# Row variance on one core: whole rows per engine and deferred aggregation instead of split rows and a combine chain

## The chip, the core and the metric

The kernel runs on one NeuronCore of a Trainium2 chip. Times are device microseconds of that core, from the start of the program to its end. A profiled execution mostly shows a span 1.7 to 1.9 us shorter than that time. The engines that matter are DVE (VectorE), ACT (ScalarE), POOL (GpSimd), the queue of SP (SyncE), which issues the loads, and the 16 DMA engines that carry them.

## The reference

```python
# x: (32, 512, 1024) float32
mean_sq = np.mean(x**2, axis=-1)
sq_mean = np.mean(x, axis=-1)**2
return (mean_sq - sq_mean).astype(np.float32)
```

This is the variance of each of 16384 rows of 1024 numbers. The input is 67.1 MB and the output 64 KB.

## The kernel before

The rows are spread over 128 partitions, so each partition has 128 rows ("row t" below means 128 rows at once, 512 KB). Row groups arrive in tiles of 1 to 8 rows through five buffers. The groups are small at both ends of the run.

```python
segs = [1, 1, 2, 4] + [8] * 11 + [4] * 5 + [2] * 4 + [1] * 4
xin = ctx.enter_context(tc.tile_pool(name="xin", bufs=5))
...
for si, js in enumerate(segs):
    x_tile = xin.tile([P, JMAX, D], fp32)
    nc.sync.dma_start(out=x_tile[:, 0:js, :], in_=...)
    for j in range(js):
        t = t0 + j
        row = x_tile[:, j, :]
        if t % 2 == 0:      # split row: ACT 656 columns, DVE 368
            nc.scalar.activation(... row[:, 0:GA], func=Square, accum_out=ssqA_buf[:, t:t+1])
            nc.scalar.activation(... row[:, 0:GA], func=Copy,   accum_out=sumA_buf[:, t:t+1])
            nc.vector.bn_stats(out=stats[:, 0, :], in_=row[:, GA:D])
            nc.vector.bn_aggr(out=mv_buf[:, t, :], in_=stats[:, 0:1, :])
        else:               # whole row on DVE
            nc.vector.bn_stats(out=stats[:, 0, :], in_=row[:, 0:HO])
            nc.vector.bn_stats(out=stats[:, 1, :], in_=row[:, HO:D])
            nc.vector.bn_aggr(out=mv_buf[:, t, :], in_=stats)
    # after rows 64 and 112: combine(prev_cp, cp)
nc.sync.dma_start(out=out_v[:, 0:prev_cp], in_=var_buf[:, 0:prev_cp])
combine(prev_cp, T)         # 6 DVE and 2 ACT operations in a chain
nc.sync.dma_start(out=out_v[:, prev_cp:T], in_=var_buf[:, prev_cp:T])
```

`combine` turns DVE's mean and variance of its part, and ACT's sums of the other part, into the variance of the row.

Of the kernel before, what the change touches and what calls it, by code (L numbers as in the profile page):

```python
# [1 line left out]

# [4 lines left out]


@with_exitstack  # L10
def kernel(
    ctx: ExitStack,
    tc: tile.TileContext,
    x: bass.AP,
    out: bass.AP,
):
    nc = tc.nc
    fp32 = mybir.dt.float32
    P = nc.NUM_PARTITIONS

    x_flat = x.flatten_outer_dims()
    N, D = x_flat.shape
    assert N % P == 0
    T = N // P

    xv = x_flat.rearrange("(p t) d -> t p d", t=T)
    out_v = out.rearrange("a b -> (a b)").rearrange("(p t) -> p t", t=T)

    JMAX = 8
    segs = [1, 1, 2, 4] + [8] * 11 + [4] * 5 + [2] * 4 + [1] * 4  # L30
    assert sum(segs) == T

    GA = 656
    NBE = D - GA
    assert NBE <= 512 and NBE % 2 == 0
    HO = D // 2
    assert HO <= 512

    xin = ctx.enter_context(tc.tile_pool(name="xin", bufs=5))
    sq = ctx.enter_context(tc.tile_pool(name="sq", bufs=2))  # L40
    stats_pool = ctx.enter_context(tc.tile_pool(name="stats_pool", bufs=4))
    accs = ctx.enter_context(tc.tile_pool(name="accs", bufs=1))

    sumA_buf = accs.tile([P, T], fp32)
    ssqA_buf = accs.tile([P, T], fp32)
    nbw_buf = accs.tile([P, T], fp32)
    mv_buf = accs.tile([P, T, 2], fp32)
    eb_buf = accs.tile([P, T], fp32)
    ebw_buf = accs.tile([P, T], fp32)
    msqB_buf = accs.tile([P, T], fp32)  # L50
    mw_buf = accs.tile([P, T], fp32)
    ssq_tot = accs.tile([P, T], fp32)
    sum_tot = accs.tile([P, T], fp32)
    sq_mean = accs.tile([P, T], fp32)
    var_buf = accs.tile([P, T], fp32)

    nc.gpsimd.memset(sumA_buf, 0.0)  # L57
    nc.gpsimd.memset(ssqA_buf, 0.0)  # L58
    nbw_v = nbw_buf.rearrange("p (a b) -> p a b", b=2)
    nc.gpsimd.memset(nbw_v[:, :, 0], float(NBE))  # L60
    nc.gpsimd.memset(nbw_v[:, :, 1], float(D))  # L61

    inv_d = 1.0 / D

    def combine(c0, c1):
        sl = slice(c0, c1)
        meanB = mv_buf[:, sl, 0]
        varB = mv_buf[:, sl, 1]
        nc.scalar.activation(  # L69
            out=msqB_buf[:, sl],  # L70
            in_=meanB,
            func=mybir.ActivationFunctionType.Square,
        )
        nc.vector.tensor_add(out=eb_buf[:, sl], in0=varB, in1=msqB_buf[:, sl])  # L74
        nc.vector.tensor_mul(out=ebw_buf[:, sl], in0=eb_buf[:, sl], in1=nbw_buf[:, sl])  # L75
        nc.vector.tensor_add(  # L76
            out=ssq_tot[:, sl], in0=ebw_buf[:, sl], in1=ssqA_buf[:, sl]
        )
        nc.vector.tensor_mul(out=mw_buf[:, sl], in0=meanB, in1=nbw_buf[:, sl])  # L79
        nc.vector.tensor_add(out=sum_tot[:, sl], in0=mw_buf[:, sl], in1=sumA_buf[:, sl])  # L80
        nc.scalar.activation(  # L81
            out=sq_mean[:, sl],
            in_=sum_tot[:, sl],
            func=mybir.ActivationFunctionType.Square,
            scale=inv_d,
        )
        nc.vector.scalar_tensor_tensor(  # L87
            out=var_buf[:, sl],
            in0=ssq_tot[:, sl],
            scalar=inv_d,  # L90
            in1=sq_mean[:, sl],
            op0=mybir.AluOpType.mult,
            op1=mybir.AluOpType.subtract,
        )

    CHECKPOINTS = [64, 112]

    t0 = 0
    prev_cp = 0
    for si, js in enumerate(segs):  # L100
        x_tile = xin.tile([P, JMAX, D], fp32)
        nc.sync.dma_start(  # L102
            out=x_tile[:, 0:js, :], in_=xv[t0 : t0 + js].transpose([1, 0, 2])
        )

        for j in range(js):
            t = t0 + j
            row = x_tile[:, j, :]

            if t % 2 == 0:  # L110
                sq_scr = sq.tile([P, GA], fp32)
                nc.scalar.activation(  # L112
                    out=sq_scr,
                    in_=row[:, 0:GA],
                    func=mybir.ActivationFunctionType.Square,
                    accum_out=ssqA_buf[:, t : t + 1],
                )
                cp_scr = sq.tile([P, GA], fp32)
                nc.scalar.activation(  # L119
                    out=cp_scr,  # L120
                    in_=row[:, 0:GA],
                    func=mybir.ActivationFunctionType.Copy,
                    accum_out=sumA_buf[:, t : t + 1],
                )

                stats = stats_pool.tile([P, 2, nc.vector.BN_STATS_DIM], fp32)
                nc.vector.bn_stats(out=stats[:, 0, :], in_=row[:, GA:D])  # L127
                nc.vector.bn_aggr(out=mv_buf[:, t, :], in_=stats[:, 0:1, :])  # L128
            else:
                stats = stats_pool.tile([P, 2, nc.vector.BN_STATS_DIM], fp32)  # L130
                nc.vector.bn_stats(out=stats[:, 0, :], in_=row[:, 0:HO])  # L131
                nc.vector.bn_stats(out=stats[:, 1, :], in_=row[:, HO:D])  # L132
                nc.vector.bn_aggr(out=mv_buf[:, t, :], in_=stats)  # L133
        t0 += js

        while CHECKPOINTS and t0 >= CHECKPOINTS[0]:
            cp = CHECKPOINTS.pop(0)
            combine(prev_cp, cp)
            prev_cp = cp

    nc.sync.dma_start(out=out_v[:, 0:prev_cp], in_=var_buf[:, 0:prev_cp])

    combine(prev_cp, T)
    nc.sync.dma_start(out=out_v[:, prev_cp:T], in_=var_buf[:, prev_cp:T])


# [1 line left out]
_INS = ['x']  # L148
_OUTS = [((32, 512), 'float32')]


# [23 lines left out]
```

## Time and profile before

| | before |
|---|---|
| time, median of the 5 first runs | 169.03 us (168.85 to 169.26) |
| span of the profiled execution | 167.3 us |
| DVE busy, ACT busy | 73%, 59% |
| last input load landed | 162.07 us |
| last output issued | 164.93 us |

The next lines are from the profile page of the kernel before: busy time of each engine with its share of the span and its instruction count, then the DMA queues (packets, MB, share of 16 engines' span), then the shares of the chain that ended last.

```profile
DVE 121.9 (73%) x338; ACT 98.9 (59%) x263; POOL 0.7 (0%) x8
...
q1 hardware_dynamic: 4320, 67.18, 94.7%
q14 instruction: 5, 0.04, 0.1%
...
DMA 83%; DVE 14%; SPq 1%; issue 0%; DVEq 0%
```

None of the computing engines is full, and the chain is DMA for 83% of its length. The second queue, "q14 instruction", is easy to overlook: five packets of 8192 bytes each, with which engines fetch their next instructions while they run. The trace dates them at 38.0, 47.6, 95.9, 116.3 and 150.6 us.

The next view is the table by stretches of the kernel before. Its columns are the stretch, its length, busy us (and instructions) of DVE, ACT and POOL, the TensorE clock, the mean busy share of the 16 DMA engines, and GB/s.

```profile
20.00:155.00 135.00, 105.34 (x293) 85.16 (x229) 0.00 (x0) 1.00 1.00 429
155.00:157.00 2.00, 1.58 (x5) 1.21 (x4) 0.00 (x0) 1.00 1.02 406
157.00:158.00 1.00, 0.93 (x2) 0.87 (x3) 0.00 (x0) 1.00 0.87 324
158.00:159.00 1.00, 1.00 (x4) 1.00 (x3) 0.00 (x0) 1.00 0.84 332
159.00:160.00 1.00, 0.93 (x4) 1.00 (x4) 0.00 (x0) 1.00 0.66 243
160.00:161.00 1.00, 0.96 (x3) 0.27 (x3) 0.00 (x0) 1.00 0.08 32
161.00:162.00 1.00, 0.72 (x3) 1.00 (x3) 0.00 (x0) 1.00 0.04 16
```

Up to 155 us all 16 DMA engines are busy at 429 GB/s. After 160 us a share of 0.04 to 0.08 remains, which is about one engine of sixteen (1/16 = 0.06). A single engine is still carrying its part of the last rows while 15 have finished.

The end of the timeline of the kernel before follows (start us, duration us, engine, line, operation, output and input). L131 to L133 are the statistics of the last row; L69 to L87 are `combine`; L144 is the output.

```profile
162.09 0.69 DVE L131 BATCH_NORM_STATS2 stats<-x_tile 128x6 f32<-128x512 f32 x1 [0.34 <-DMA x_tile<-in_x_dram]
...
163.42 0.21 DVE L133 BATCH_NORM_AGGREGATE mv_buf<-stats 128x2 f32<-128x12 f32 x1
...
163.66 0.18 DVE L79 TENSOR_TENSOR mw_buf<-mv_buf,nbw_buf 128x16 f32<-128x16 f32 x1
...
164.24 0.18 DVE L75 TENSOR_TENSOR ebw_buf<-eb_buf,nbw_buf 128x16 f32<-128x16 f32 x1
...
164.73 0.17 DVE L87 SCALAR_TENSOR_TENSOR var_buf<-ssq_tot,sq_mean 128x16 f32<-128x16 f32 x1
164.93 0.34 SPq L144 DMA_DIRECT2D out_dram<-var_buf  x1
```

DVE is waiting for the last row (the bracket says so). From there to the output's issue it takes 2.84 us, a chain of DVE operations with two short ACT operations of `combine` in it.

The trace also records when each DMA engine's share of a load landed. The following extract is worked out from those records. It shows four loads of the kernel before: the middle of the 16 engines, the third from last, the second from last, and the last.

```
time order     median   third-last  second-last   last    last minus third-last
one at 62 us    61.71      61.99        62.08     62.41   0.42
one at 102 us  100.57     100.84       100.95    102.23   1.39
rows 120, 121  151.93     152.20       153.01    154.55   2.35
row 127        159.78     160.14       160.54    162.07   1.93
```

One engine falls further and further behind. A tile is usable only when its last engine has landed, so that engine sets the end of the input.

### The profile page before, as it was taken

To read this page: it belongs to the slowest core of one execution; us is meant where nothing else is said; L and a number is where in the kernel's file an instruction comes from. 1 tells how busy PE (TensorE), PEld (TensorE's weight loads), DVE (VectorE), ACT (ScalarE), POOL (GpSimd) and SP (SyncE) were. 2 spreads that over 40 slices of the span, in tenths; PEclk is the share of its full clock that TensorE was granted. 3 is DMA by queue.
4 is the path that set the end of the run, shared out by engine and by line. 5 is a ranking of instruction groups with operands and counts; after the bars stand their busy time and mean duration, and the time that the engine had idled before them with its cause. 6 is when DMAs were issued, how large, how long until landed. Compare 5 with 4: busy or idle time off the path is not lost.

```text
span 167.3 us, 735 instructions
## 1 busy us (share of the span) xinstructions
DVE 121.9 (73%) x338; ACT 98.9 (59%) x263; POOL 0.7 (0%) x8
## 2 busy tenths in 40 slices
DVE  0547149496794949679497965949599997998883
ACT  0637049193773919376492935829289755694761
POOL 1000000000000000000000000000000000000000
DMA  5999898999999999999999999999999999999910
GB/s 183 404 439 478 384 486 384 478 400 433 439 417 462 400 470 392 470 400 454 423 415 462 394 470 392 478 400 449 388 427 427 435 431 427 405 421 410 370 73 2
DMA packets 4325, 67.22 MB, mean 402 GB/s; under 512 B 736, under 2 KB 736, under 8 KB 1504
## 3 DMA queue, kind: packets, MB, share of 16 engines
q1 hardware_dynamic: 4320, 67.18, 94.7%
q14 instruction: 5, 0.04, 0.1%
HBM read 67.11 MB, written 0.07 MB: 402 GB/s over the span
## 4 chain that ended last, share of the span: by engine, by line
DMA 83%; DVE 14%; SPq 1%; issue 0%; DVEq 0%
DMA x_tile<-in_x_dram 83%; DVE stats L132 5%; DVE stats L131 5%; DVE stats L127 3%; DVE mv_buf L133 1%; DVE mv_buf L128 1%; SPq L102 1%; DVE ssq_tot L76 0%; DVE ebw_buf L75 0%; DVE mw_buf L79 0%; DVE var_buf L87 0%; DVE sum_tot L80 0%; DVE eb_buf L74 0%; DVEq L87 0%; DVEq L80 0%
## 5 line engine op out<-in xcount | busy, mean ns | idle before, releaser
L112 ACT ACTIVATE sq_scr<-x_tile 128x656 f32<-128x656 f32 x64 | 47.3, 739 | 56.8 <-DMA x_tile<-in_x_dram 56.7
L127 DVE BATCH_NORM_STATS2 stats<-x_tile 128x6 f32<-128x368 f32 x64 | 34.0, 531 | 40.3 <-DMA x_tile<-in_x_dram 40.2
L119 ACT ACTIVATE cp_scr<-x_tile 128x656 f32<-128x656 f32 x64 | 46.9, 733 | 0.0
L131 DVE BATCH_NORM_STATS2 stats<-x_tile 128x6 f32<-128x512 f32 x64 | 41.9, 654 | 0.9 <-DMA x_tile<-in_x_dram 0.8
L132 DVE BATCH_NORM_STATS2 stats<-x_tile 128x6 f32<-128x512 f32 x64 | 42.3, 661 | 0.0
L133 DVE BATCH_NORM_AGGREGATE mv_buf<-stats 128x2 f32<-128x12 f32 x64 | 12.7, 198 | 0.8
L119 ACT ACTIVATION_READ_ACCUMULATOR cp_scr<-x_tile 128x1 f32 x64 | 11.9, 187 | 0.0
L112 ACT ACTIVATION_READ_ACCUMULATOR sq_scr<-x_tile 128x1 f32 x64 | 11.9, 186 | 0.0
L128 DVE BATCH_NORM_AGGREGATE mv_buf<-stats 128x2 f32<-128x6 f32 x64 | 10.6, 166 | 0.1
L112 ACT ACT_TABLE_LOAD x1 | 1.3, 1283 | 4.5 <-DMA x_tile<-in_x_dram 4.5
L69 ACT ACTIVATE msqB_buf<-mv_buf 128x64 f32<-128x64 f32 (+2 forms) x3 | 0.7, 240 | 3.3 <-DVE mv_buf L133 3.3
L81 ACT ACTIVATE sq_mean<-sum_tot 128x64 f32<-128x64 f32 (+2 forms) x3 | 0.7, 238 | 1.0 <-DVE sum_tot L80 1.0
L87 DVE SCALAR_TENSOR_TENSOR var_buf<-ssq_tot,sq_mean 128x64 f32<-128x64 f32 (+2 forms) x3 | 0.6, 204 | 0.3
L80 DVE TENSOR_TENSOR sum_tot<-mw_buf,sumA_buf 128x64 f32<-128x64 f32 (+2 forms) x3 | 0.6, 203 | 0.3
L79 DVE TENSOR_TENSOR mw_buf<-mv_buf,nbw_buf 128x64 f32<-128x64 f32 (+2 forms) x3 | 0.6, 203 | 0.2
L75 DVE TENSOR_TENSOR ebw_buf<-eb_buf,nbw_buf 128x64 f32<-128x64 f32 (+2 forms) x3 | 0.6, 203 | 0.1
L76 DVE TENSOR_TENSOR ssq_tot<-ebw_buf,ssqA_buf 128x64 f32<-128x64 f32 (+2 forms) x3 | 0.6, 203 | 0.1
L74 DVE TENSOR_TENSOR eb_buf<-mv_buf,msqB_buf 128x64 f32<-128x64 f32 (+2 forms) x3 | 0.6, 197 | 0.0
L57 POOL MEMSET sumA_buf<- 128x128 f32 x1 | 0.2, 205 | 0.3 <-POOLq L159 0.3
L58 POOL MEMSET ssqA_buf<- 128x128 f32 x1 | 0.2, 205 | 0.0
L60 POOL MEMSET nbw_buf<- 128x64 f32 x1 | 0.2, 155 | 0.0
L61 POOL MEMSET nbw_buf<- 128x64 f32 x1 | 0.2, 155 | 0.0
(4 smaller groups left out, 0.4 us busy)
## 6 DMA issues: line engine op xcount, KB each, us to landing
x_tile<-in_x_dram SPq DMA_DIRECT2D x11, 4096.0 KB, 41.8
x_tile<-in_x_dram SPq DMA_DIRECT2D x6, 2048.0 KB, 24.5
x_tile<-in_x_dram SPq DMA_DIRECT2D x5, 1024.0 KB, 14.6
x_tile<-in_x_dram SPq DMA_DIRECT2D x6, 512.0 KB, 6.2
out_dram<-var_buf SPq DMA_DIRECT2D x1, 56.0 KB, 5.4
out_dram<-var_buf SPq DMA_DIRECT2D x1, 8.0 KB, 1.4
```

The lines of the kernel that those rows point to most:

```text
L69: nc.scalar.activation(out=msqB_buf[:, sl], in_=meanB, func=mybir.ActivationFunctionType.Square,)
L74: nc.vector.tensor_add(out=eb_buf[:, sl], in0=varB, in1=msqB_buf[:, sl])
L75: nc.vector.tensor_mul(out=ebw_buf[:, sl], in0=eb_buf[:, sl], in1=nbw_buf[:, sl])
L81: nc.scalar.activation(out=sq_mean[:, sl], in_=sum_tot[:, sl], func=mybir.ActivationFunctionType.Square, scale=inv_d,)
L102: nc.sync.dma_start(out=x_tile[:, 0:js, :], in_=xv[t0 : t0 + js].transpose([1, 0, 2]))
L112: nc.scalar.activation(out=sq_scr, in_=row[:, 0:GA], func=mybir.ActivationFunctionType.Square, accum_out=ssqA_buf[:, t : t + 1],)
L119: nc.scalar.activation(out=cp_scr, in_=row[:, 0:GA], func=mybir.ActivationFunctionType.Copy, accum_out=sumA_buf[:, t : t + 1],)
L127: nc.vector.bn_stats(out=stats[:, 0, :], in_=row[:, GA:D])
L128: nc.vector.bn_aggr(out=mv_buf[:, t, :], in_=stats[:, 0:1, :])
L131: nc.vector.bn_stats(out=stats[:, 0, :], in_=row[:, 0:HO])
L132: nc.vector.bn_stats(out=stats[:, 1, :], in_=row[:, HO:D])
L133: nc.vector.bn_aggr(out=mv_buf[:, t, :], in_=stats)
```

## The change

The change has several parts. Every row now belongs to one engine: ACT has rows 0 to 8 and every third row, DVE has the rest. DVE keeps only raw bn_stats results for most rows, and POOL aggregates them later. For rows from 120 on DVE aggregates straight into the output buffer, so that no combine chain remains behind the last row. Rows 126 and 127 are loaded in halves. The intent is less work on DVE and a shorter end. The diff is cut to its core:

```diff
+    def is_scalar_row(t):
+        return t < 9 or (t % 3 == 2)
...
-    nc.gpsimd.memset(sumA_buf, 0.0)          # and the other buffers of combine
...
+    W = accs.tile([P, 2, T], fp32)           # [:, 0] mean, [:, 1] variance
...
     def combine(c0, c1):                     # now for the ACT rows alone
-        (two ACT and six DVE operations on all rows)
...
+            nc.scalar.activation(out=m2_buf[:, sl], in_=W[:, 0, sl], func=Square)
+            eng = nc.vector if c1 == T else nc.gpsimd
+            eng.tensor_sub(out=var_v[:, sl], in0=msq_buf[:, sl], in1=m2_buf[:, sl])
+    AGG = 120
+    def aggregate(c0, c1):                   # DVE rows, on POOL
+        for r in (0, 1):
+            (13 POOL operations on rows r, r+3, ...)
...
-    CHECKPOINTS = [64, 112]
+    CHECKPOINTS = [63, 111]
...
+        cuts = [(0, HO), (HO, D)] if t0 >= 126 else [(0, D)]
...
-            if t % 2 == 0:
+            if is_scalar_row(t):
-                (ACT: Square and Copy of 656 columns; DVE: bn_stats of 368, bn_aggr)
+                (ACT: Square and Copy of all 1024 columns, scaled)
             else:
                 nc.vector.bn_stats(out=stats[:, 0, :], in_=row[:, 0:HO])
                 nc.vector.bn_stats(out=stats[:, 1, :], in_=row[:, HO:D])
-                nc.vector.bn_aggr(out=mv_buf[:, t, :], in_=stats)
+                if t >= AGG:
+                    nc.vector.bn_aggr(out=W[:, :, t], in_=stats)
...
+        if t0 == AGG:
+            aggregate(prev_cp, AGG)
```

More of the change, by code (lines that the diff above doesn't have):

```diff
@@ L31 @@
     assert sum(segs) == T
-    GA = 656
-    NBE = D - GA
-    assert NBE <= 512 and NBE % 2 == 0
+    def is_scalar_row(t):
+        return t < 9 or (t % 3 == 2)
     HO = D // 2
     assert HO <= 512
+    inv_d = 1.0 / D
+    inv_sqrt_d = D ** -0.5
+    assert inv_sqrt_d * inv_sqrt_d == inv_d
     xin = ctx.enter_context(tc.tile_pool(name="xin", bufs=5))
     sq = ctx.enter_context(tc.tile_pool(name="sq", bufs=2))
-    stats_pool = ctx.enter_context(tc.tile_pool(name="stats_pool", bufs=4))
     accs = ctx.enter_context(tc.tile_pool(name="accs", bufs=1))
-    sumA_buf = accs.tile([P, T], fp32)
@@ L45 @@
-    ssqA_buf = accs.tile([P, T], fp32)
-    nbw_buf = accs.tile([P, T], fp32)
-    mv_buf = accs.tile([P, T, 2], fp32)
-    eb_buf = accs.tile([P, T], fp32)
-    ebw_buf = accs.tile([P, T], fp32)
-    msqB_buf = accs.tile([P, T], fp32)
-    mw_buf = accs.tile([P, T], fp32)
-    ssq_tot = accs.tile([P, T], fp32)
-    sum_tot = accs.tile([P, T], fp32)
-    sq_mean = accs.tile([P, T], fp32)
-    var_buf = accs.tile([P, T], fp32)
-    nc.gpsimd.memset(sumA_buf, 0.0)
-    nc.gpsimd.memset(ssqA_buf, 0.0)
@@ L59 @@
-    nbw_v = nbw_buf.rearrange("p (a b) -> p a b", b=2)
-    nc.gpsimd.memset(nbw_v[:, :, 0], float(NBE))
-    nc.gpsimd.memset(nbw_v[:, :, 1], float(D))
-    inv_d = 1.0 / D
-    def combine(c0, c1):
-        sl = slice(c0, c1)
-        meanB = mv_buf[:, sl, 0]
-        varB = mv_buf[:, sl, 1]
-        nc.scalar.activation(
-            out=msqB_buf[:, sl],
-            in_=meanB,
-            func=mybir.ActivationFunctionType.Square,
-        )
-        nc.vector.tensor_add(out=eb_buf[:, sl], in0=varB, in1=msqB_buf[:, sl])
-        nc.vector.tensor_mul(out=ebw_buf[:, sl], in0=eb_buf[:, sl], in1=nbw_buf[:, sl])
-        nc.vector.tensor_add(
-            out=ssq_tot[:, sl], in0=ebw_buf[:, sl], in1=ssqA_buf[:, sl]
-        )
-        nc.vector.tensor_mul(out=mw_buf[:, sl], in0=meanB, in1=nbw_buf[:, sl])
-        nc.vector.tensor_add(out=sum_tot[:, sl], in0=mw_buf[:, sl], in1=sumA_buf[:, sl])
-        nc.scalar.activation(
-            out=sq_mean[:, sl],
-            in_=sum_tot[:, sl],
-            func=mybir.ActivationFunctionType.Square,
-            scale=inv_d,
-        )
-        nc.vector.scalar_tensor_tensor(
-            out=var_buf[:, sl],
-            in0=ssq_tot[:, sl],
-            scalar=inv_d,
-            in1=sq_mean[:, sl],
-            op0=mybir.AluOpType.mult,
-            op1=mybir.AluOpType.subtract,
-        )
@@ L96 @@
-    CHECKPOINTS = [64, 112]
+    W = accs.tile([P, 2, T], fp32)
+    msq_buf = accs.tile([P, T], fp32)
+    m2_buf = accs.tile([P, T], fp32)
+    var_v = W[:, 1, :]
+    def combine(c0, c1):
+        slices = []
+        if c0 < 9:
+            slices.append(slice(c0, min(c1, 9)))
+            c0 = 9
+        if c0 < c1:
+            s = c0 + (2 - c0 % 3) % 3
+            if s < c1:
+                slices.append(slice(s, c1, 3))
+        for sl in slices:
+            nc.scalar.activation(
+                out=m2_buf[:, sl],
+                in_=W[:, 0, sl],
+                func=mybir.ActivationFunctionType.Square,
+            )
+            eng = nc.vector if c1 == T else nc.gpsimd
+            eng.tensor_sub(
+                out=var_v[:, sl], in0=msq_buf[:, sl], in1=m2_buf[:, sl]
+            )
@@ new lines @@
+    keep = accs.tile([P, T, 4, 3], fp32)
+    g4 = accs.tile([P, T, 4], fp32)
+    g2 = accs.tile([P, T, 2], fp32)
+    h2 = accs.tile([P, T, 2], fp32)
+    s1 = accs.tile([P, T], fp32)
+    s2 = accs.tile([P, T], fp32)
+    AGG = 120
+    def aggregate(c0, c1):
+        g = nc.gpsimd
+        for r in (0, 1):
+            a = max(c0, 9)
+            a += (r - a) % 3
+            sl = slice(a, c1, 3)
+            mean = keep[:, sl, :, 1]
+            m2 = keep[:, sl, :, 2]
+            g.tensor_add(out=g2[:, sl], in0=mean[:, :, 0:2], in1=mean[:, :, 2:4])
+            g.tensor_add(out=s1[:, sl], in0=g2[:, sl, 0], in1=g2[:, sl, 1])
+            g.tensor_mul(out=s1[:, sl], in0=s1[:, sl], in1=s1[:, sl])
+            g.tensor_mul(out=g4[:, sl], in0=mean, in1=mean)
+            g.tensor_add(out=h2[:, sl], in0=g4[:, sl, 0:2], in1=g4[:, sl, 2:4])
+            g.tensor_add(out=s2[:, sl], in0=h2[:, sl, 0], in1=h2[:, sl, 1])
+            g.tensor_scalar_mul(out=s2[:, sl], in0=s2[:, sl], scalar1=0.25)
+            g.tensor_scalar_mul(out=s1[:, sl], in0=s1[:, sl], scalar1=0.0625)
+            g.tensor_sub(out=s2[:, sl], in0=s2[:, sl], in1=s1[:, sl])
+            g.tensor_add(out=g2[:, sl], in0=m2[:, :, 0:2], in1=m2[:, :, 2:4])
+            g.tensor_add(out=s1[:, sl], in0=g2[:, sl, 0], in1=g2[:, sl, 1])
+            g.tensor_scalar_mul(out=s1[:, sl], in0=s1[:, sl], scalar1=inv_d)
+            g.tensor_add(out=var_v[:, sl], in0=s1[:, sl], in1=s2[:, sl])
@@ L98 @@
+    CHECKPOINTS = [63, 111]
     t0 = 0
     prev_cp = 0
-    for si, js in enumerate(segs):
+    for js in segs:
         x_tile = xin.tile([P, JMAX, D], fp32)
-        nc.sync.dma_start(
-            out=x_tile[:, 0:js, :], in_=xv[t0 : t0 + js].transpose([1, 0, 2])
-        )
+        cuts = [(0, HO), (HO, D)] if t0 >= 126 else [(0, D)]
+        for lo, hi in cuts:
+            nc.sync.dma_start(
+                out=x_tile[:, 0:js, lo:hi],
+                in_=xv[t0 : t0 + js, :, lo:hi].transpose([1, 0, 2]),
+            )
@@ L108 @@
             row = x_tile[:, j, :]
-            if t % 2 == 0:
-                sq_scr = sq.tile([P, GA], fp32)
+            if is_scalar_row(t):
+                sq_scr = sq.tile([P, D], fp32)
                 nc.scalar.activation(
                     out=sq_scr,
-                    in_=row[:, 0:GA],
+                    in_=row,
                     func=mybir.ActivationFunctionType.Square,
-                    accum_out=ssqA_buf[:, t : t + 1],
+                    scale=inv_sqrt_d,
+                    accum_out=msq_buf[:, t : t + 1],
                 )
-                cp_scr = sq.tile([P, GA], fp32)
+                cp_scr = sq.tile([P, D], fp32)
                 nc.scalar.activation(
                     out=cp_scr,
-                    in_=row[:, 0:GA],
+                    in_=row,
                     func=mybir.ActivationFunctionType.Copy,
-                    accum_out=sumA_buf[:, t : t + 1],
-                )
-                stats = stats_pool.tile([P, 2, nc.vector.BN_STATS_DIM], fp32)
-                nc.vector.bn_stats(out=stats[:, 0, :], in_=row[:, GA:D])
-                nc.vector.bn_aggr(out=mv_buf[:, t, :], in_=stats[:, 0:1, :])
+                    scale=inv_d,
+                    accum_out=W[:, 0, t : t + 1],
+                )
             else:
-                stats = stats_pool.tile([P, 2, nc.vector.BN_STATS_DIM], fp32)
+                stats = keep[:, t].rearrange("p (a b) c -> p a (b c)", b=2)
                 nc.vector.bn_stats(out=stats[:, 0, :], in_=row[:, 0:HO])
                 nc.vector.bn_stats(out=stats[:, 1, :], in_=row[:, HO:D])
-                nc.vector.bn_aggr(out=mv_buf[:, t, :], in_=stats)
+                if t >= AGG:
+                    nc.vector.bn_aggr(out=W[:, :, t], in_=stats)
         t0 += js
+        if t0 == AGG:
+            aggregate(prev_cp, AGG)
         while CHECKPOINTS and t0 >= CHECKPOINTS[0]:
@@ L138 @@
             combine(prev_cp, cp)
+            aggregate(prev_cp, cp)
             prev_cp = cp
-    nc.sync.dma_start(out=out_v[:, 0:prev_cp], in_=var_buf[:, 0:prev_cp])
+    nc.sync.dma_start(out=out_v[:, 0:prev_cp], in_=var_v[:, 0:prev_cp])
     combine(prev_cp, T)
-    nc.sync.dma_start(out=out_v[:, prev_cp:T], in_=var_buf[:, prev_cp:T])
+    nc.sync.dma_start(out=out_v[:, prev_cp:T], in_=var_v[:, prev_cp:T])
 _INS = ['x']
```

## The prediction

> **What bounds the kernel now.** The input transfer. In the table by stretches the DMA share is 1.00 from 20 to 155 us at about 430 GB/s, while DVE is busy 73% and ACT 59% of the span; 83% of the chain of waits is DMA. Eight-row tiles land every 9.7 us and cost DVE about 7.1 us. Work saved inside the stream is worth nothing; only the tail counts.
>
> **The tail, before.** Timeline: last row lands 162.09; two 512-wide bn_stats and bn_aggr to 163.63; combine chain to 164.90 (six DVE operations); output issued 164.93; end 167.3. So 2.84 us lie between last landing and output issue.
>
> Landing records of the 16 DMA engines: for the last row 15 engines landed by 160.56, most by 160.2, one at 162.09. That one lags 0.3 us at 62 us, 1.3 at 102, 2.3 at 152. The steps follow the instruction fetches (instruction queue, five in the run: 38.0, 47.7, 96.0, 116.3, 150.7 us). The Trainium skill, "DMA: Bandwidth & Descriptors", section "Queues, rings and completion order", has the runtime's internal row share the 16 engines with data; these lags agree. I read three fetches as DVE's (about 340 instructions), two as ACT's.
>
> **What the change does.**
> - Middle: DVE keeps about 80 whole rows (about 108 us), ACT 48. An ACT pass of 1024 is estimated at 0.73 us (traced, 656 wide) + 368 x 0.833 ns (rate from the skill's "ScalarE: Activation LUTs", "What ACT_TABLE_LOAD costs") = 1.04 us, so about 100 us in all. Both stay under the stream: 0. Rows 0 to 8 on ACT alone release buffers up to 5 us later, but at least 16 rows (19 us) stay queued: 0.
> - bn_aggr moves to POOL as 78 small operations, of which this trace has none. My guess is 0.25 to 0.40 us each with the wait; the last 26 start near 152 us (row 118's statistics) and end at 159 to 162.5, just in time.
> - DVE's instructions halve (338 to about 167): one fetch instead of three; ACT one; POOL perhaps one, late. The straggler's lag should fall from 1.5 us to well under 1: last landing 160.6 to 161.2, worth about 1.1 us.
> - After the last landing only one bn_stats (0.69), bn_aggr (0.21) and wake-ups remain, 1.0 us instead of 2.84. But rows 124, 126 and 127 are all DVE's at 1.4 us each, so DVE carries some backlog: I take 1.4. Worth about 1.4 us.
> - Rows 120 and 121 are both DVE's and release row 127's buffer after 2.7 instead of 1.8 us, offset by their earlier landing: 0 to 0.3 us lost. Halved last loads (2 KB runs, two more issues of 0.33 us): 0.1 us lost.
>
> Sum: about -2.5 us, all in the last 8 us of the span.
>
> **Predicted: 166.5 us**, 8 in 10 between 165.5 and 168.3. Faster by over 2% (under 165.65): 0.15; within 2%: 0.83; slower: 0.02.
>
> **What would show each step.** Stretches: DMA share 1.00 from 20 to 155 us. Instruction queue: three or fewer packets. Landing records: spread of the last transfer under 1 us. Chain of waits: ends in bn_stats and bn_aggr of row 127, no combine. Timeline: output issued near 162.4; last POOL operation before that.
>
> **What would make it wrong.** POOL operations over 0.38 us: the output waits for POOL and the gain shrinks or turns to a loss. A late POOL instruction fetch makes a new straggler. Row 127's loads issue so late that all DMA engines run dry (up to 0.9 us). If DVE carries no backlog, the gain reaches 3.3 us and touches 2%.

## The result and the profile after

Ratios here and below are the mean time of one kernel's runs over that of the other's runs of the same rounds, so they are not quite the ratio of the medians quoted beside them.

| | before | after |
|---|---|---|
| time, median | 169.01 us (16 runs) | 165.96 us (9 runs) |
| ratio | | 0.9823, interval 0.9807 to 0.9839 |
| span of the profiled execution | 167.3 us | 164.2 us |
| last input load landed | 162.07 us | 160.71 us |
| last output issued | 164.93 us | 161.94 us |

The span lost 3.1 us: 1.36 from the earlier last landing, 1.63 between it and the issue of the output (2.86 became 1.23), and 0.11 after it (2.37 became 2.26).

The same page lines of the changed kernel:

```profile
DVE 97.9 (60%) x167; ACT 104.2 (63%) x197; POOL 17.9 (11%) x85
...
q1 hardware_dynamic: 4608, 67.18, 96.6%
q14 instruction: 4, 0.03, 0.0%
...
DMA 82%; DVE 8%; ACT 8%; issue 0%; SPq 0%; ACTq 0%
```

DVE lost half its instructions and 24 us of busy time, and yet the busy time is not where the 3 us come from. The table by stretches of the changed kernel shows why:

```profile
20.00:155.00 135.00, 91.33 (x153) 83.36 (x159) 16.62 (x76) 1.00 1.00 429
155.00:157.00 2.00, 1.95 (x5) 1.40 (x3) 1.05 (x5) 1.00 1.02 399
157.00:158.00 1.00, 0.98 (x3) 0.79 (x2) 0.00 (x0) 1.00 1.02 369
158.00:159.00 1.00, 0.80 (x3) 0.82 (x1) 0.00 (x0) 1.00 1.02 378
159.00:160.00 1.00, 1.00 (x2) 1.00 (x3) 0.00 (x0) 1.00 0.48 160
160.00:161.00 1.00, 0.97 (x5) 0.57 (x3) 0.00 (x0) 1.00 0.03 11
161.00:162.00 1.00, 0.84 (x3) 0.00 (x0) 0.00 (x0) 1.00 0.00 0
```

In the stream, 20 to 155 us, DVE has 14 us less to do and the DMA moves the same 429 GB/s at share 1.00. From 157 on the traffic ends sooner, and the remnant after 160 us is smaller.

The end of the timeline of the changed kernel (L138 and L139 are the two bn_stats of a row, L141 is bn_aggr, L67 the last subtraction for the ACT rows, L155 the output):

```profile
158.79 0.69 DVE L138 BATCH_NORM_STATS2 keep<-x_tile 128x6 f32<-128x512 f32 x1 [0.17 <-DMA x_tile<-in_x_dram]
...
160.33 0.64 DVE L138 BATCH_NORM_STATS2 keep<-x_tile 128x6 f32<-128x512 f32 x1
...
160.88 0.15 DVE L67 TENSOR_TENSOR W<-msq_buf,m_buf 128x5 f32<-128x5 f32 x1
160.95 0.69 DVE L139 BATCH_NORM_STATS2 keep<-x_tile 128x6 f32<-128x512 f32 x1
161.67 0.21 DVE L141 BATCH_NORM_AGGREGATE W<-keep 128x2 f32<-128x12 f32 x1
161.94 0.34 SPq L155 DMA_DIRECT2D out_dram<-W  x1
```

The last half row landed at 160.71, but its bn_stats starts at 160.95, since DVE is still 0.24 us behind with the rows before. Then bn_aggr and the output follow, and no combine chain. The last POOL work in the same timeline, for rows 111 to 118, starts and ends well before that:

```profile
150.54 0.21 POOL L88 TENSOR_TENSOR g<-keep 128x6 f32<-128x6 f32 x1 [1.82 <-DVE keep L139]
...
156.21 0.20 POOL L100 TENSOR_TENSOR W<-s,s 128x3 f32<-128x3 f32 x1
```

These 26 operations take 5.9 us, 0.23 us each (156.41 less 150.54, over 26).

### The profile page after: what moved, and what is told of

Same layout as the page of the kernel before. It is cut to its first block, busy times and chain, and to the rows that moved or that the text cites. A ratio compares the mean times of both kernels' runs of the same rounds, so it can differ in the third digit from the quotient of the medians.

```text
span 164.2 us, 568 instructions
## 1 busy us (share of the span) xinstructions
DVE 97.9 (60%) x167; ACT 104.2 (63%) x197; POOL 17.9 (11%) x85
## 4 chain that ended last, share of the span: by engine, by line
DMA 82%; DVE 8%; ACT 8%; issue 0%; SPq 0%; ACTq 0%
DMA x_tile<-in_x_dram 82%; DVE keep L138 4%; DVE keep L139 4%; ACT sq_scr L121 4%; ACT cp_scr L129 4%; DVE W L141 0%; DVE W L67 0%; SPq L110 0%; ACTq L121 0%
## 5 line engine op out<-in xcount | busy, mean ns | idle before, releaser
L138 DVE BATCH_NORM_STATS2 keep<-x_tile 128x6 f32<-128x512 f32 x80 | 54.4, 680 | 63.8 <-DMA x_tile<-in_x_dram 63.7
L121 ACT ACTIVATE sq_scr<-x_tile 128x1024 f32<-128x1024 f32 x48 | 50.3, 1048 | 55.6 <-DMA x_tile<-in_x_dram 55.6
L139 DVE BATCH_NORM_STATS2 keep<-x_tile 128x6 f32<-128x512 f32 x80 | 54.1, 676 | 0.0
L129 ACT ACTIVATE cp_scr<-x_tile 128x1024 f32<-128x1024 f32 x48 | 49.9, 1040 | 0.0
L88 POOL TENSOR_TENSOR g<-keep 128x36 f32<-128x36 f32 (+2 forms) x6 | 1.6, 260 | 106.0 <-DVE keep L139 106.0
L121 ACT ACTIVATION_READ_ACCUMULATOR sq_scr<-x_tile 128x1 f32 x48 | 9.0, 187 | 0.0
L129 ACT ACTIVATION_READ_ACCUMULATOR cp_scr<-x_tile 128x1 f32 x48 | 9.0, 187 | 0.0
L67 POOL TENSOR_TENSOR W<-msq_buf,m_buf 128x9 f32<-128x9 f32 (+2 forms) x3 | 0.7, 232 | 29.3 <-ACT m_buf L61 29.3
L95 POOL TENSOR_SCALAR s<-s 128x18 f32<-128x18 f32 (+2 forms) x6 | 1.6, 267 | 0.5
L91 POOL TENSOR_TENSOR g<-keep 128x72 f32<-128x72 f32 (+2 forms) x6 | 1.6, 274 | 0.0
L94 POOL TENSOR_SCALAR s<-s 128x18 f32<-128x18 f32 (+2 forms) x6 | 1.6, 264 | 0.5
L99 POOL TENSOR_SCALAR s<-s 128x18 f32<-128x18 f32 (+2 forms) x6 | 1.6, 262 | 0.5
L97 POOL TENSOR_TENSOR g<-keep 128x36 f32<-128x36 f32 (+2 forms) x6 | 1.5, 255 | 0.0
L100 POOL TENSOR_TENSOR W<-s,s 128x18 f32<-128x18 f32 (+2 forms) x6 | 1.4, 228 | 0.5
L141 DVE BATCH_NORM_AGGREGATE W<-keep 128x2 f32<-128x12 f32 x6 | 1.2, 208 | 0.2
L98 POOL TENSOR_TENSOR s<-g 128x18 f32<-128x18 f32 (+2 forms) x6 | 1.3, 214 | 0.5
L89 POOL TENSOR_TENSOR s<-g 128x18 f32<-128x18 f32 (+2 forms) x6 | 1.3, 214 | 0.0
```

The lines of the kernel that those rows point to most:

```text
L88: g.tensor_add(out=g2[:, sl], in0=mean[:, :, 0:2], in1=mean[:, :, 2:4])
L91: g.tensor_mul(out=g4[:, sl], in0=mean, in1=mean)
L94: g.tensor_scalar_mul(out=s2[:, sl], in0=s2[:, sl], scalar1=0.25)
L95: g.tensor_scalar_mul(out=s1[:, sl], in0=s1[:, sl], scalar1=0.0625)
L97: g.tensor_add(out=g2[:, sl], in0=m2[:, :, 0:2], in1=m2[:, :, 2:4])
L99: g.tensor_scalar_mul(out=s1[:, sl], in0=s1[:, sl], scalar1=inv_d)
```

## The experiments

**Theory A.** Most of the earlier landing comes from DVE having fewer instructions. Each fetch is an 8192-byte packet on one of the 16 DMA engines, and the fetches of one instruction stream keep burdening one engine. The trace allows a cost to be read. In the kernel before, the fetch at 95.9 us took 0.33 us, and one data packet right behind it took 1875 ns where a packet of its size (32768 bytes) takes 1213: together about 1.0 us lost on one engine. Read this way, the five fetches cost 0.92, 0.66, 1.00, 0.69 and 0.97 us. At those of 38, 96 and 151 us DVE had passed 56, 183 and 311 entries of the trace, 127 and 128 apart, so I read the three dear ones as DVE's. Those three alone come to 2.9 us on one engine, and the straggler is 1.9 to 2.4 us late. The changed kernel has one such fetch (67 us, 0.84) and three of 0.65 to 0.68.

**Theory B.** The halved last loads and the new tail bring everything, and fetches do not matter.

**Theory C.** The last landing was late because the load of row 127 was issued late (156.4 us), behind a buffer that DVE had to release. The drop of the DMA share to 0.84 at 158 us in the kernel before speaks for it.

In the landing column below, "last" is the last DMA engine of the last input load, from the profiled execution. The column "lag" is, for the load that landed near 152 us, the last engine's landing minus the median one's. Times and ratios to the kernel before are from 5 rounds (4 to 6 runs each); the first two rows have 16 and 9 runs.

| run | fetches in the stream: their cost in us | lag | median engine, last | time us | ratio (interval) |
|---|---|---|---|---|---|
| before | 0.92, 0.66, 1.00, 0.69, 0.97 | 2.62 | 159.78, 162.07 | 169.01 | 1 |
| after | 0.65, 0.84, 0.68, 0.66 | 1.03 | 159.73, 160.71 | 165.96 | 0.9823 (0.9807 to 0.9839) |
| dve_filler | 0.69, 0.99, 0.99, 0.99, 0.68, 0.66 | 2.77 | 160.28, 161.81 | 167.09 | 0.9891 (0.9878 to 0.9905) |
| pool_filler | 0.69, 0.67, 0.99, 0.66, 0.65, 0.68 | 1.93 | 159.42, 160.96 | 166.17 | 0.9836 (0.9823 to 0.9850) |
| before_no_aggr | 0.69, 0.99, 0.69, 0.97 | 2.00 | 159.11, 160.98 | 167.94 | 0.9941 (0.9928 to 0.9953) |
| before_new_tail | 0.99, 0.69, 0.99, 0.69, 0.99 | 2.81 | 160.42, 161.97 | 167.18 | 0.9895 (0.9880 to 0.9910) |
| after_old_tail | 0.65, 1.00, 0.68, 0.66 | 0.96 | 159.69, 160.65 | 167.93 | 0.9940 (0.9919 to 0.9961) |
| before_tailbuf | 0.93, 0.67, 1.00, 0.69, 0.97 | 2.67 | 160.12, 162.72 | 169.06 | 1.0004 (0.9984 to 1.0024) |
| after_no_pool | 0.66, 0.99, 0.98, 0.68 | 1.36 | 159.86, 161.16 | 166.62 | 0.9850 (0.9831 to 0.9869) |
| after_whole_loads | 0.65, 0.92, 0.68, 0.66 | 1.13 | 159.42, 160.50 | 166.51 | 0.9854 (0.9833 to 0.9875) |
| lean | 0.99, 0.69 | 1.40 | 159.65, 160.95 | 166.34 | 0.9830 (0.9809 to 0.9850) |
| after_again | 0.69, 0.92, 0.68, 0.66 | 0.95 | 159.79, 160.65 | 165.97 | 0.9824 (0.9804 to 0.9844) |
| after_tailbuf | 0.63, 0.85, 0.68, 0.66 | 0.83 | 159.81, 160.59 | 166.00 | 0.9820 (0.9800 to 0.9840) |
| lean_tailbuf | 0.89, 0.69 | 0.25 | 159.74, 160.02 | 166.09 | 0.9821 (0.9802 to 0.9841) |

All results were correct but that of before_no_aggr. The landings are of one execution each. Their streams do not start level: the first 8-row tile landed (median engine) between 22.4 and 23.4 us. So differences of landings between runs under about half a microsecond say little; the lag does not have this flaw, since it compares engines within one load.

The lag also tests theory A inside one trace. In the kernel before, the lag of the last engine steps from 0.32 to 0.71 us at the fetch of 38 us, to 1.65 at that of 96 and to 2.6 at that of 151, and is level in between. At 96 the lag of the second-last engine stays at 0.37, and no engine is left at 0.71: the same engine was hit again. The cheaper fetch at 116 us lifts the second-last engine from 0.37 to 1.04. dve_filler shows the same steps (0.78, 1.76, 2.75) at its three dear fetches. So fetches do pile up on one engine; that the dear ones are DVE's is still read from the counts of instructions.

### dve_filler: give DVE its instructions back

```diff
                 nc.vector.bn_stats(out=stats[:, 1, :], in_=row[:, HO:D])
+                if t < 108:
+                    for _ in range(3):
+                        nc.vector.tensor_copy(out=junk[:, 0:1], in_=keep[:, t, 0, 0:1])
```

> The changed kernel, with three one-column copies on DVE after each of its rows up to row 107 (about 200 instructions, in time that DVE spends waiting), so that DVE again has about as many instructions as before the change. Theory A (each fetch of 8192 bytes of instructions holds one of the 16 DMA engines for 0.65 to 1.0 us, and the last landing waits for the engine with most fetches): fetches in the run rise from 4 to 6, one engine lags by 1.3 to 2 us more, last landing goes from 160.67 to 161.8 to 162.5 us, time from 165.96 to about 167.3. Theory B (the earlier last landing of the changed kernel comes from its halved last loads and earlier issue, fetches do not matter): last landing stays at 160.7, time 166.0 within 0.3.

The page of this run shows the instruction count and the queue:

```profile
DVE 116.8 (71%) x365; ACT 104.1 (63%) x197; POOL 17.8 (11%) x85
...
q14 instruction: 6, 0.05, 0.1%
```

All six packets of the instruction queue are fetches of 8192 bytes, and three of them cost 0.99 us each. The last landing moved from 160.71 to 161.81, as expected, and the time rose by 1.1 us, a little less than expected. The copies work on one column and the tail is that of the changed kernel: the output is issued at 163.01, 1.20 us after the last landing (1.23 in the changed kernel). Theory B is out. The rival that a busier DVE released buffers later does not explain a lag of 2.77 us against 1.03 within one load near 152 us; before_tailbuf below issues loads early and keeps its lag. Not all of the lag reaches the end directly: at the last load it is 1.53. The last load was issued at 157.65 (156.43 in the changed kernel) and the DMA share from 157 to 158 us was 0.53 (1.02), so here part of the delay came through the other engines running short of loads.

### pool_filler: the same dose on another engine

```diff
+                        nc.gpsimd.tensor_copy(out=junk[:, 0:1], in_=keep[:, t, 0, 0:1])   # four per DVE row
```

> The changed kernel, with four one-column copies on POOL for each DVE row up to row 107 (about 260 instructions on an engine that otherwise waits). Theory A: two more instruction fetches, now POOL's; whichever DMA engine serves them becomes the straggler: last landing 161.5 to 162.3, time 166.8 to 167.5, though DVE and ACT do exactly what they did. Theory B: time 166.0 within 0.3. A third possibility, that DVE's own load sets the landing, also predicts no change here.

There were six fetches again, but the time rose by only 0.2 us (the intervals overlap) and the last landing is 160.96. This is a miss for theory A as I had written it. It had taken any two more fetches to be worth about 1 us. The additional ones here cost 0.65 to 0.67 us instead of 0.99. They did make a new last engine, as theory A said: the lag steps to 1.24 us at the fetch of 89 us and to 1.9 at that of 130, against 1.03 near 152 us in the changed kernel. But little of these 0.9 us arrived. At the last load the lag was 1.54, and the median engine landed at 159.42, 0.31 earlier than in the changed kernel. The third possibility of the expectation, that DVE's own load sets the landing, would fit this run's time too; against it stand the steps of the lag, which come at the fetches although DVE does no more here than in the changed kernel. Why so little reached the end is open, so the lag of the most burdened engine does not give the time one to one. The trace names neither the DMA engine of a packet nor the stream of a fetch, so that these are POOL's is inferred.

### before_no_aggr: take instructions from DVE in the kernel before

```diff
-                nc.vector.bn_aggr(out=mv_buf[:, t, :], in_=stats)
+                if t >= 112:
+                    nc.vector.bn_aggr(out=mv_buf[:, t, :], in_=stats)
```

(The same was done for the split rows, and the unwritten buffer was cleared at the start.)

> The kernel before, without bn_aggr for rows 0 to 111 (112 DVE instructions fewer; the result is wrong on purpose for those rows, the tail is untouched). Theory A: DVE's fetches fall from 3 to 2, the straggler loses about 0.9 to 1.0 us, last landing 161.1 to 161.3 instead of 162.09, tail after it still 2.84 us, time 168.0 to 168.3. Theory B: last landing 162.1, time 169.0 within 0.3.

With 226 DVE instructions there are four fetches, two of them dear. The last landing is 160.98, 1.09 earlier, and the output follows 2.85 us later (163.83), as before. The lag near 152 us is 2.00 instead of 2.62. The time fell by 1.0 us, slightly more than expected. So the earlier landing can be had without any change to the tail.

### before_new_tail and after_old_tail: each half of the change alone

before_new_tail keeps the old stream and takes over the new treatment of rows 112 to 127; after_old_tail is its mirror image, with rows 111 to 127 in the old way. The core of the first:

```diff
-            if t % 2 == 0:
+            if t >= TAIL and t % 3 == 2:
+                (ACT: whole row into msq_buf and W, as in the changed kernel)
+            elif t >= TAIL:
+                (two bn_stats, then bn_aggr into W[:, :, t])
+            elif t % 2 == 0:
...
-    combine(prev_cp, T)
+    combine_tail()          # square and subtract for the ACT rows only
```

> The kernel before up to row 111, with the changed kernel's treatment of rows 112 to 127 (whole rows per engine, bn_aggr straight into the output buffer, halved last loads, no combine chain after the last row), without POOL. DVE still has about 330 instructions. Theory A: still 5 fetches, last landing 161.8 to 162.2, then 1.0 to 1.3 us to the output's issue: time 167.2 to 167.6, so about 1.7 of the 3.05 us. Theory B: the halved loads and the tail bring everything: 166.0 to 166.4.

> The changed kernel up to row 110, with the earlier kernel's treatment of rows 111 to 127 (split rows on ACT and DVE, combine chain after the last row, whole loads). Theory A: DVE's fetches stay at one before the last landing (a second may come after it), last landing 160.6 to 161.0, then 2.8 us to the output's issue: time 167.6 to 168.0, so about 1.2 of the 3.05 us. Theory B (landing is due to the halved loads): last landing near 162, time 168.7 to 169.0.

Both came as theory A had them. The new tail alone, with five fetches and the last landing at 161.97, brings 1.77 us. The new stream alone, with whole loads and the old combine chain, has its last landing at 160.65 and brings 1.17 us. Together that is 2.94, against 3.05 for the whole change (medians). Halved loads are not needed for the early landing.

The timeline of after_old_tail shows the old chain at nearly its old length behind the early landing, 160.68 to 163.60 (2.92 us; 2.84 in the kernel before):

```profile
160.68 0.69 DVE L195 BATCH_NORM_STATS2 stats<-x_tile 128x6 f32<-128x512 f32 x1 [0.38 <-DMA x_tile<-in_x_dram]
...
163.60 0.34 SPq L232 DMA_DIRECT2D out_dram<-var_buf  x1
```

### before_tailbuf: issue the last loads early

```diff
+    xlast = ctx.enter_context(tc.tile_pool(name="xlast", bufs=4))
...
-        x_tile = xin.tile([P, JMAX, D], fp32)
+        if t0 < 124:
+            x_tile = xin.tile([P, JMAX, D], fp32)
+        else:
+            x_tile = xlast.tile([P, 1, D], fp32)
```

> The kernel before, with four own small buffers for rows 124 to 127, so that the last four loads wait for no consumer and are issued early. Nothing else changes. Theory A (the last landing waits for the one engine that served most fetches): the 15 other engines no longer run short between 157.5 and 158.5 us and land row 127 by about 159.9 instead of 160.2 to 160.6, but the straggler still lands at 161.8 to 162.1: time 168.7 to 169.1. Theory C (the last landing was late because its load was issued late, at 156.4 us): last landing 160.5 to 161, time 167.6 to 168.

The table by stretches of the kernel before, and then of this run, around the dip:

```profile
157.50:158.00 0.50, 0.50 (x2) 0.50 (x3) 0.00 (x0) 1.00 0.66 221
158.00:158.50 0.50, 0.50 (x3) 0.50 (x1) 0.00 (x0) 1.00 0.70 262
158.50:159.00 0.50, 0.50 (x2) 0.50 (x3) 0.00 (x0) 1.00 0.98 401
```

```profile
157.50:158.00 0.50, 0.30 (x1) 0.24 (x1) 0.00 (x0) 1.00 1.02 410
158.00:158.50 0.50, 0.50 (x2) 0.50 (x2) 0.00 (x0) 1.00 0.99 393
158.50:159.00 0.50, 0.50 (x3) 0.50 (x3) 0.00 (x0) 1.00 1.04 418
```

The dip is gone and the time is unchanged (ratio 1.0004). The last landing of this execution is 162.72, 2.3 us after the third from last (160.42). It is later than expected, probably because the whole stream of this execution, the slowest of its six, ran late: its first 8-row tile landed at 23.80, against 23.14 in the kernel before. Theory C is out: the dip was harmless, because the engines that ran short were not the one that was last.

### after_no_pool, after_whole_loads: what the other parts are worth

The first aggregates every DVE row on DVE and drops POOL; the second drops the halved loads.

```diff
-                if t >= AGG:
+                if True:                        # and no calls of aggregate()
```

```diff
-        cuts = [(0, HO), (HO, D)] if t0 >= 126 else [(0, D)]
+        cuts = [(0, D)]
```

> The changed kernel with bn_aggr on DVE for every DVE row, nothing on POOL (74 DVE instructions more, 78 POOL operations fewer). If work in the stream is worth nothing, only the fetches move: DVE from one to two, POOL from one to none. Theory A: the engine that serves DVE's fetches gains 0.8 us, last landing 160.9 to 161.5, time 166.1 to 166.7. If POOL relieved DVE of time that matters: 167 or more. Theory B: 166.0.

> The changed kernel with rows 126 and 127 loaded whole. Stream ends 0.1 to 0.2 us earlier (2 KB packets take 84 ns, 4 KB 159), but both bn_stats of the last row start only after it has landed: output issued 0.4 to 0.6 us later, time 166.3 to 166.6. Theory B: last landing moves back towards 162, time 167.2.

The times fell in the expected ranges: about 0.5 us slower than the changed kernel by the ratios (0.9850 and 0.9854 against 0.9823). The 74 bn_aggr on DVE cost nothing in the stream; they brought the second dear fetch, at which the lag steps from 0.39 to 1.34 us, and the last landing at 161.16. The halves cost a little transfer time (the last landing of the whole loads is 160.50, 0.21 earlier), but they let DVE start on row 126 before all of it is there (158.79 against 159.29); the output is issued 0.35 us earlier than with whole loads, where 0.4 to 0.6 was expected. The intervals of these two touch or overlap that of the changed kernel, so the sizes are rough.

### lean, after_tailbuf, lean_tailbuf: attempts to go further

lean gives ACT every third row from the start (42 instead of 48) and handles both DVE rows of each three in one POOL pattern, which halves POOL's operations.

```diff
-        return t < 9 or (t % 3 == 2)
+        return t % 3 == 2
...
-        for r in (0, 1):
-            sl = slice(a, c1, 3)
+        kv = keep[:, c0:c1].rearrange("p (k r) f c -> p k r f c", r=3)[:, :, 0:2]
```

> A version meant to beat both: rows with t mod 3 = 2 on ACT from the start (42 rows instead of 48), both DVE rows of each three aggregated by one POOL pattern (39 operations instead of 78), so that ACT and POOL cross one fetch each less. Theory A: fetches before the last landing fall from 4 to 2, last landing 160.2 to 160.5, time 165.4 to 165.8. Theory B: 166.0 within 0.2.

> The changed kernel unaltered, on the same chip as the next two, as their yardstick: 165.8 to 166.2 us.

> The changed kernel with own small buffers for rows 124 to 127. Its engines were busy to 159 us already, so the earlier issue gains at most the issue order: last landing 160.3 to 160.7, time 165.7 to 166.1. Theory C would have it gain 0.5 us or more.

> The lean version (2 fetches in the stream instead of 4) with the same own buffers. Its one DVE fetch still makes the straggler, so no more than 0 to 0.4 us below the changed kernel: 165.5 to 166.2. If the number of fetches over all engines counted, rather than those of the worst engine, it would be 165.2 or less.

lean got its two fetches, but not the time: 166.34 us (165.80 to 166.80), with the last landing at 160.95. Its one DVE fetch (0.99) still makes one engine last: the lag steps there from 0.68 to 1.38. The saved fetches were not worthless: in the changed kernel the lag steps from 0.52 to 1.04 at 144 us, at a fetch that lean does not have there. But the engines do not start level: in the first 8-row tile the last landing is already 0.68 us behind the median in lean (23.50 and 22.82), 0.22 in the changed kernel and 0.55 in its repetition. Own buffers for the last rows change nothing here either. lean_tailbuf had a profiled span of 163.4 us with a last landing of 160.02 and a lag of 0.25, but its time, 166.09 us, is that of the changed kernel. Span and time must not be mixed here. The spans of all runs of lean and lean_tailbuf are 163.4 to 164.4 us, those of after_again 164.0 to 164.5; but lean's versions spend 2.0 to 2.6 us outside the span, and the changed kernel 1.75 to 1.85. So part of the gain was there and was lost outside the span. The two lean traces have one more fetch after the span's end (at 166.62 and 165.68 us), and no other trace has one there; that it is the cause was not tested. None of the three beats the changed kernel beyond noise.

## Why the prediction was right

The predicted time was 166.5 us; 165.96 was measured, inside the range, and "within 2%" is what happened. Both gains came by the paths that were forecast, but each was larger than forecast and the forecast losses were not seen, so the errors add up in one direction (2.5 us predicted, 3.05 measured) and the result lies 0.46 us above the lower end of the range. Point by point:

- **Work in the stream is worth nothing: right.** DMA share 1.00 and 429 GB/s in both kernels while DVE lost 14 us there. after_no_pool gave DVE 74 operations back and lost only what the second fetch explains.
- **Fewer fetches, earlier landing: right, and shown** by dve_filler (+1.1 us) and before_no_aggr (-1.0 us). I had put 1.1 us on it; 1.36 us were measured in the profile, and 1.17 us with that half alone. The prediction's lags of the straggler (0.3, 1.3, 2.3) were taken against different neighbours; one measure gives 0.42, 1.39 and 2.35.
- **Number of fetches: wrong.** I said three or fewer, the queue shows four in the stream. ACT still crossed two, and POOL one. These are the cheaper ones (0.65 to 0.68), but not harmless: in the profiled execution the fetch of 144 us, the second of the two that I read as ACT's, is the one that sets the final lag (0.52 to 1.04 us). The prediction had counted one fetch of ACT, not two.
- **Shorter tail: right, undersized.** I took 1.4 us from landing to issue, allowing for DVE's backlog; it was 1.23, of which 0.24 is backlog.
- **POOL: right in outcome, too dear.** I guessed 0.25 to 0.40 us per operation, ending at 159 to 162.5. They took 0.23 us and ended at 156.4. The Trainium skill ("GPSIMD Engine Reference", "3.1 Elementwise — side-by-side cycle accounting") gives 4497 ns for an addition of 2048 elements. Nothing that long runs here; the operations of 3 to 72 elements took 0.20 to 0.31 us, so these sizes are mostly fixed cost.
- **Losses of 0.1 to 0.4 us (later buffer release, 2 KB runs): not seen as net losses.** 2 KB packets do take 84 ns where a 4 KB one takes 159, but after_whole_loads is slower, not faster. after_tailbuf shows that the late release costs nothing.
- **ACT and DVE totals: ACT right, DVE too high.** An ACT pass of 1024 took 1.04 us as estimated (104 us in all, where about 100 were forecast); DVE was busy 98 us, not 108, because a bn_stats that follows another starts 0.6 us after it.

Still open: which DMA engine serves which instruction stream; why the fetches that I read as DVE's cost 0.84 to 1.00 us and most others 0.63 to 0.69; why pool_filler's lag hardly reached the end; what lean loses outside its span; and why the engines start uneven. The changed kernel's end is close to being bound by DVE, which works on six of the last eight rows with almost no pause from 153.05 us on. Giving ACT one more of those rows was not tried.

## What to carry to other kernels

When the 16 DMA engines are full, a load is as late as its most delayed engine. So look at the spread of a load's landings, not only at the mean GB/s. Long unrolled instruction streams are not free in such a kernel: each 128 or so DVE instructions cost one DMA engine about 1 us here (how much of it reaches the end differed: 1.1 us in dve_filler, 0.2 for POOL's in pool_filler), and dropping instructions in time that DVE spent idle was worth a third or more of the gain. What follows the last landing is paid in full, so let it be one short operation per engine and move every reduction over all rows in front of it.

## What the Trainium skill lacked or had wrong

- "Runtime: NRT & Kernel Launch", section "Instruction fetch mechanics", says that a sequencer fetches its next instructions over a DMA queue of its own and calls the cost mostly hidden. In a DMA-bound kernel it is not always hidden: 0.63 to 1.0 us of one DMA engine per fetch, and 1.0 to 1.1 us of the kernel's time where DVE's fetches changed in number (before_no_aggr, dve_filler), though only 0.2 us in pool_filler.
- The same section gives refills of 16 KiB (256 instructions). In these traces each fetch is one packet of 8192 bytes, and DVE's come at 56, 183 and 311 entries of its trace.
- "DMA: Bandwidth & Descriptors", section "Queues, rings and completion order", says that the queue rows share the engines packet by packet. The trace agrees, but the page does not give the price. Beside the fetch's own 0.31 to 0.33 us, the data packet right behind it took 0.32 to 0.66 us longer than usual.
- "GPSIMD Engine Reference", section "3.1 Elementwise — side-by-side cycle accounting", has no figure for operations of a few elements. Here 26 dependent ones of 3 to 12 elements took 0.23 us each, wait included.
- No page that I read speaks of uneven starts of the DMA engines: 0.2 to 0.9 us between the median and the last landing of the first 8-row tile, different from run to run.
